# Two heads' value products by turns into the two halves of one PSUM bank, in both causal attentions of a two-layer trunk

## The chip, the core and the metric

One core of a Trainium2 chip runs the whole forward pass in one launch. The metric is device time in microseconds (us), the median of several executions. TensorE (PE in the profile, with PEld for its weight loads), VectorE (DVE), ScalarE (ACT) and GpSimd (POOL) have instruction streams of their own and wait for each other by semaphores. SyncE (SP) issues the loads from memory.

## The reference

Two layers over 512 tokens of width 1024. Each layer is a half-weighted feed-forward, a mixer, an attention over 256 memory tokens, and a second half-weighted feed-forward. The mixers hold the two causal attentions that are changed here: layer 0 a stick-breaking attention (8 heads of width 64, beside a gated branch), layer 1 a softmax attention with low-rank projections (16 heads, value width 64).

```python
for layer in range(DEPTH):
    x = x + 0.5 * _swiglu(_rmsnorm(x, ffn_pre_norm[layer]), ...)
    h = _rmsnorm(x, mix_norm[layer])
    if layer % 2 == 0:
        x = x + _even_mixer(h, ...)      # stick-breaking attention | gated branch, @ w_out
    else:
        x = x + _mla_mixer(h, ...)       # causal softmax attention, @ w_out
    x = x + _memory_cross_attention(...)
    x = x + 0.5 * _swiglu(_rmsnorm(x, ffn_post_norm[layer]), ...)

# stick breaking, per query block, strict = key position < query position
log_stay = jnp.where(strict, jax.nn.log_sigmoid(-z), 0.0)
log_rest = lax.cumsum(log_stay, axis=3, reverse=True) - log_stay
w = jnp.where(strict, jnp.exp(jax.nn.log_sigmoid(z) + log_rest), 0.0)
return jnp.einsum('bhqk,bkhd->bqhd', w, v)
# softmax
p = jax.nn.softmax(jnp.where(causal, sc, -jnp.inf), axis=-1)
return jnp.einsum('bhqk,bkhd->bqhd', p, v)
```

The last line of each attention is the value product that the change issues in another order.

## The kernel before

The residual stream lies on chip with features on partitions, as eight tiles of 128 x 512. Most products run as three passes of fp32r operands that were split into a high and a low part (`mm3`, lines 98 to 100). Weights come in granules (`gran`): a load, a rounded copy on ACT (line 79) and a difference on DVE or POOL (line 83).

The value products are different. Their operands are plain fp32, one product per key block j, four for a head, with 512, 384, 256 and 128 columns, since key block j meets only the queries from block j on. The stationary operand is v of one head, 128 keys x 64 features; what streams are the attention weights, keys on partitions. The result has 64 partitions. Heads of even number write partitions 0 to 63 of the accumulator `av`, heads of odd number partitions 64 to 127. A pair of heads fills the bank, and then ACT and DVE split it into the operands of the output projection (`obh`, `obl` in layer 0; `hh`, `hl` in layer 1).

**Layer 0, `stick`.** Per head `h`: `scores(h)` puts z for three units of key blocks into three PSUM banks; DVE adds the mask (line 359); ACT takes Abs, Exp and Ln (lines 416 to 418); DVE makes the softplus (line 419) and splits it into `th` and `tl` (lines 81, 83). `weights(h)` adds products of `th` and `tl` with triangular constants on TensorE (line 433), and ACT takes the Exp (line 436), which gives the weights. Between the two, `take(4)` twice draws eight steps of a filler: products that wait for nothing (the next pair's q and k, later half of the output projection). The value products of head h - 1 (line 444) stand between the two `take(4)` of step h. The filler is used up at the end.

**Layer 1, `mla_attn`.** In step n: `scores(n)` with the softmax (mask line 760, maximum 765, Exp 771, scaling 777), `weights(n - 1)`, which turns the weights by TensorE transposes (line 790) and copies them out of PSUM (ACT line 795 for units 0 and 1, DVE line 797 for unit 2), `turn` of head n + 2 (line 703), and `values(n - 1)` (line 808). Filler projections stand between them in steps 0 to 8. From there on early parts of the output projection fill in. All that the step issues on TensorE is held in written order by `queued()`, save products of the next stage.

A scheduler sets the order in which each engine's stream is written down: where the code does not bind it, it places an instruction by its own estimate of times. So a change on TensorE can also change the order on ACT and DVE.

Of the kernel before, what the change touches and what calls it, by code (L numbers as in the profile page):

```python
# [26 lines left out]
class Trunk:  # L27
    """The residual stream xT lives feature-major on chip; every product runs as
    three fp32r passes over operands split exactly into a high and a low part."""

    def __init__(self, ctx, tc, a, stop=None):
# [10 lines left out]
        # PSUM: two banks stay through all phases, which start in their own banks and end in these two,  # L42
        # so that no phase's first product waits for the last one's evacuation
# [3 lines left out]
    def queued(self):  # L47
        """What the block issues on the tensor engine comes behind what it had before."""
        return self.tc.issue_after(self.pe.ins)
# [9 lines left out]
    # ---------------------------------------------------------------- pieces  # L59
    def constants(self):  # L60
# [3 lines left out]
        # the first weights ahead of x: their split takes longer  # L64
# [10 lines left out]
    def split(self, hi, lo, src, eng_hi="act", eng_lo="dve"):  # L75
        """hi = src rounded to the multiplier's width, lo = src - hi (exact)."""
        nc = self.nc
        if eng_hi == "act":
            nc.scalar.copy(out=hi, in_=src)  # L79
        else:  # L80
            nc.vector.tensor_copy(out=hi, in_=src)
        e = nc.vector if eng_lo == "dve" else nc.gpsimd
        e.tensor_tensor(out=lo, in0=src, in1=hi.bitcast(F32), op=ALU.subtract)  # L83

    def gran(self, src, kt, cols, lo="pool"):
        """A weight granule [128, kt*cols] loaded and split."""
# [15 lines left out]
    def rsqrt(self, ssq, n, scale, eps, shape=None):  # L102
        """1/sqrt(ssq*scale + eps) on [128, n] by bit estimate and three Newton steps."""
# [13 lines left out]
    def prep(self, g, f):  # L117
        """Split gain*x_f for the next norm's consumers."""
# [12 lines left out]
    def squares(self, f):  # L131
        """Add the squares of x_f to the sums of the next norm."""
# [9 lines left out]
    def stats(self, pp, tag, bufs=None, bc=False):  # L142
        """rstd of every token: rc [128, NT] by token tile, and, if bc, rbc broadcast over partitions."""
# [28 lines left out]
    def out_half(self, ps, w, src, kh, first):  # L172
        """One half of the contraction of a pair of out_proj's output tiles, in steps."""
# [7 lines left out]
    def out_proj(self, pp, tag, w, src, order, g, begun=None):  # L181
        """x += src @ w by pairs of output tiles; w in granules [pair*2 + khalf] of [128, 4, 256].
        begun: accumulators that hold the first half already."""
# [15 lines left out]
    # ---------------------------------------------------------------- FFN  # L199
# [43 lines left out]
    # ---------------------------------------------------------------- token-major products  # L243
    def tok_chunk(self, pp, tag, grans):
        """h @ w for 256 columns, token-major: two banks of [128, 2, 256]."""
# [11 lines left out]
    # ---------------------------------------------------------------- layer 0's mixer  # L257
# [15 lines left out]
    def sgu(self, p, pp, v, og):  # L273
# [8 lines left out]
        # only s <= t mixes: partition s, free t  # L282
# [50 lines left out]
    def stick(self, p, pp, v, ob, src):  # L333
        """Stick-breaking attention, scores as [key, query]: causal blocks only."""
        nc, a = self.nc, self.a
        # key block -> (unit, column of its queries j*128.. in the unit); units are one bank each
# [9 lines left out]
        # -1 where row key >= column key  # L346
# [3 lines left out]
        # far below every score where key >= query: no softplus there, and no weight  # L350
# [10 lines left out]
        def proj(qk, pr, s):  # L361
            """q or k of a pair of heads, in steps."""
# [18 lines left out]
        def filler():  # L381
            """Products that wait for nothing, between the steps of the heads: the next pairs' q and k,
            and the part of the output projection that is fed by the gate."""
# [13 lines left out]
        def scores(h):  # L397
            """z of a head and the split softplus of its causal part."""
# [3 lines left out]
            for u in range(3):  # L402
# [8 lines left out]
                x2 = self.t(p, [P, n], f"t2{u}", bufs=2)  # L411
# [12 lines left out]
        def weights(st):  # L424
            """Suffix sums of the softplus, and the weights."""
# [12 lines left out]
        def values(h, st):  # L438
            if h % 2 == 0:
                self.av = self.t(pp, [P, S], "av", bufs=1)  # L440
            r = slice(h % 2 * 64, h % 2 * 64 + 64)
            for j in range(NT):
                u, o = AT[j]
                nc.tensor.matmul(self.av[r, j * P:], lhsT=v[:, j, h * 64:(h + 1) * 64], rhs=st[u][1][:, o:o + W[j]],
                                 start=(j == 0), stop=(j == NT - 1), skip_group_check=True)
            if h % 2 == 1:
                self.split(*ob[h // 2], self.av, "act", "dve")
# [6 lines left out]
        old = None  # L454
        for h in range(8):
            st = scores(h)
            take(4)
            if old is not None:
                values(h - 1, old)
            take(4)  # L460
            weights(st)
            old = st
        values(7, old)
# [3 lines left out]
    # ---------------------------------------------------------------- layer 1's mixer  # L467
    def rope_tables(self, p, op):
        """cos and sin of positions * inv_freq for [token, tile, 16], reduced modulo 2 pi by an
        exact digit scheme, and multiplied into the q and k gains of the two rope halves."""  # L470
# [59 lines left out]
    def mla(self):  # L530
        nc, tc, a = self.nc, self.tc, self.a
        H = 16
        with ExitStack() as outer:
# [20 lines left out]
            # the late tiles take the space of the stage before, so that the early ones need not wait for it  # L554
# [6 lines left out]
    def lora(self, p, pp, c, n, ss, cT, lg, j0):  # L561
        """rmsnorm of the token-major c [128, NT, n], turned feature-major and split."""
# [56 lines left out]
    def mla_attn(self, p, pl, pp, cT, krr, skr, gqk, neg, tq, o):  # L619
# [7 lines left out]
        def norms(st):  # L627
            """rstd of the heads' k (0) and q (1) from their sums of squares."""
# [484 lines left out]
```

## Time and profile before

| | us |
|---|---|
| median of 3 runs | 2326.71 |
| lowest, highest | 2326.22, 2329.08 |
| span of the profiled execution | 2328.0 |
| TensorE busy in it | 2274.4 (98%) |
| VectorE, ScalarE, GpSimd busy | 1018.2, 875.1, 903.4 |

The profile gives no time of the profiled execution apart from its span, 2328.0 us from the first to the last instruction, 1.3 us above the median of the runs. Its granted TensorE clock has a mean of 0.995 of full speed. In the rows a busy time is a union over time, and a record of a matrix product lasts from its start to the modelled end of its pipeline, so neighbours overlap; the distance from start to start is what TensorE spends on one.

### The profile page before, as it was taken

The page shows a single profiled execution, that of the slowest core. Times are in us where ns is not written, and L with a number is a line of the kernel's source. Part 1 is how long each engine was busy: PE and PEld are TensorE (multiplying, and loading weights), DVE is VectorE, ACT ScalarE, POOL GpSimd, SP SyncE. Part 2 cuts the span into 40 slices and gives each one's busy share as a digit, 9 for nine tenths or more (in the row PEclk, how much of TensorE's full clock was granted, in tenths as well). Part 3 has the DMA queues.
Part 4 walks back from the last instruction along what each step waited for, and adds up shares of the span by engine and source line. Part 5 has one row for each costly group of instructions (what it writes and reads, how often), then busy time and mean ns, then how long its engine had stood idle before and what let it go on. Part 6 is the DMA issues. An engine that isn't in the chain of part 4 may idle for free. (4 is left out here: it accounts for less than half of the span.)

```text
span 2328.0 us, 28369 instructions
## 1 busy us (share of the span) xinstructions
PE 2274.4 (98%) x11152; PEld 1891.5 (81%) x11152; DVE 1018.2 (44%) x1830; ACT 875.1 (38%) x1448; POOL 903.4 (39%) x441
## 2 busy tenths in 40 slices
PE   7999999999999999999999999998999999999999
PEld 6888888977988788888878888897768887888887
DVE  5322433465745533133343133368886545430330
ACT  4222233355644332232332223346655443322321
POOL 4444444201242444444544444434212323445443
PEclk9999999999999999999999999999999999999999
DMA  4223323311431232332322332321103313323322
GB/s 152 92 87 113 92 82 118 92 46 47 134 110 55 83 99 81 110 100 83 108 90 83 108 100 86 99 80 57 37 19 119 127 55 91 91 79 111 100 81 92
DMA packets 67350, 208.65 MB, mean 90 GB/s; under 512 B 8592, under 2 KB 10640, under 8 KB 67216
## 3 DMA queue, kind: packets, MB, share of 16 engines
q1 hardware_dynamic: 67216, 206.83, 29.1%
q8 instruction: 88, 1.44, 0.3%
q14 instruction: 46, 0.38, 0.1%
HBM read 204.70 MB, written 2.10 MB: 89 GB/s over the span
## 5 line engine op out<-in xcount | busy, mean ns | idle before, releaser
L83 POOL TENSOR_TENSOR wl<-wr,wh 128x1024 fp32r<-128x1024 f32 (+2 forms) x382 | 850.6, 2227 | 1253.0 <-ACT wh L79 1188.8
L79 ACT CAST wh<-wr 128x1024 fp32r<-128x1024 f32 (+3 forms) x423 | 408.7, 966 | 1029.8 <-PE mm L99 540.7
L98 PE MATMUL mm<-hh,wh 128*128 128x512 f32 x1440 | 562.8, 391 | 6.6 <-ACT hh L125 6.6
L100 PE MATMUL mm<-hh,wl 128*128 128x512 f32 x1440 | 562.5, 391 | 0.9 <-POOL wl L83 0.9
L99 PE MATMUL mm<-hl,wh 128*128 128x512 f32 x1440 | 562.2, 390 | 0.5 <-DVE hl L126 0.5
L98 PEld LDWEIGHTS mm<-hh,wh 128*128 128x128 f32 x1440 | 271.5, 189 | 62.9 <-ACT hh L125 6.6
L100 PEld LDWEIGHTS mm<-hh,wl 128*128 128x128 f32 x1440 | 271.6, 189 | 57.6 <-POOL wl L83 1.3
L99 PEld LDWEIGHTS mm<-hl,wh 128*128 128x128 f32 x1440 | 271.3, 188 | 57.6 <-DVE hl L126 1.0
L98 PE MATMUL A<-ah,wh 128*128 128x512 f32 x704 | 277.4, 394 | 0.0
L100 PE MATMUL A<-ah,wl 128*128 128x512 f32 x704 | 276.0, 392 | 0.0
L99 PE MATMUL A<-al,wh 128*128 128x512 f32 x704 | 273.2, 388 | 0.0
L222 DVE TENSOR_TENSOR t<-mm,rbc 128x512 f32<-128x512 f32 x88 | 60.8, 691 | 390.5 <-PE mm L100 390.5
L234 DVE SCALAR_TENSOR_TENSOR x<-A,x 128x512 f32<-128x512 f32 x64 | 44.3, 691 | 354.3 <-PE A L100 354.3
L83 DVE TENSOR_TENSOR al<-t,ah 128x512 fp32r<-128x512 f32 x88 | 160.8, 1828 | 59.1 <-ACT ah L79 59.1
L100 PEld LDWEIGHTS A<-ah,wl 128*128 128x128 f32 x704 | 132.1, 188 | 31.0
L99 PEld LDWEIGHTS A<-al,wh 128*128 128x128 f32 x704 | 132.2, 188 | 29.6
L98 PEld LDWEIGHTS A<-ah,wh 128*128 128x128 f32 x704 | 132.3, 188 | 26.4
L220 DVE TENSOR_TENSOR t<-mm,rbc 128x512 f32<-128x512 f32 x88 | 60.9, 692 | 117.1 <-PE mm L100 110.8
L126 DVE SCALAR_TENSOR_TENSOR hl<-x,gc,hh 128x512 fp32r<-128x512 f32 x64 | 82.8, 1307 | 36.7 <-ACT hh L125 36.6
L98 PE MATMUL A<-hh,wh 128*128 128x512 f32 x224 | 91.6, 410 | 0.7 <-ACT hh L79 0.7
L99 PE MATMUL A<-hl,wh 128*128 128x512 f32 x224 | 90.0, 402 | 0.0
L100 PE MATMUL A<-hh,wl 128*128 128x512 f32 x224 | 89.8, 401 | 0.0
(322 smaller groups left out, 3260.6 us busy)
## 6 DMA issues: line engine op xcount, KB each, us to landing
wr<-in_w_gu SPq DMA_DIRECT2D x176, 512.0 KB, 3.6
wr<-in_w_dn SPq DMA_DIRECT2D x64, 384.0 KB, 3.1
wr<-in_w_dn SPq DMA_DIRECT2D x64, 320.0 KB, 2.9
wr<-in_xmem_wkv SPq DMA_DIRECT2D x32, 512.0 KB, 3.2
wr<-in_xmem_wq SPq DMA_DIRECT2D x16, 512.0 KB, 3.3
wr<-in_xmem_wo SPq DMA_DIRECT2D x16, 512.0 KB, 3.2
wr<-in_sbg_w_zv SPq DMA_DIRECT2D x12, 512.0 KB, 3.5
wr<-in_sbg_w_qk SPq DMA_DIRECT2D x8, 512.0 KB, 3.6
```

What stands on the lines that cost most here:

```text
L79: nc.scalar.copy(out=hi, in_=src)
L83: e.tensor_tensor(out=lo, in0=src, in1=hi.bitcast(F32), op=ALU.subtract)
L98: mm(out, lhsT=A[0], rhs=B[0], start=start, stop=False, skip_group_check=True)
L99: mm(out, lhsT=A[0], rhs=B[1], start=False, stop=False, skip_group_check=True)
L100: self.pe = mm(out, lhsT=A[1], rhs=B[0], start=False, stop=stop, skip_group_check=True)
L126: nc.vector.scalar_tensor_tensor(out=hl, in0=self.x[f], scalar=col, in1=hh.bitcast(F32), op0=ALU.mult, op1=ALU.subtract)
L220: nc.vector.tensor_tensor(out=t1, in0=pg, in1=self.rbc, op=ALU.mult)
L222: nc.vector.tensor_tensor(out=t2, in0=pu, in1=self.rbc, op=ALU.mult)
L234: nc.vector.scalar_tensor_tensor(out=self.x[m], in0=ps, scalar=0.5, in1=self.x[m], op0=ALU.mult, op1=ALU.add)
```

## The change

`values` now takes a pair of heads and runs the key blocks outermost: for each j the product of the even head into partitions 0 to 63, then that of the odd head into partitions 64 to 127. It runs once the weights of both heads are there: in `stick` in steps h = 2, 4, 6 and after the last, in `mla_attn` in steps n = 2, 4, ..., 16. The number, the sizes and the operands of the products stay. `t2`, the buffer that holds layer 0's weights, has three buffers and not two, since the even head's weights live a step longer.

```diff
-                x2 = self.t(p, [P, n], f"t2{u}", bufs=2)
+                x2 = self.t(p, [P, n], f"t2{u}", bufs=3)
...
-        def values(h, st):
-            if h % 2 == 0:
-                self.av = self.t(pp, [P, S], "av", bufs=1)
-            r = slice(h % 2 * 64, h % 2 * 64 + 64)
+        def values(pr, sts):
+            av = self.t(pp, [P, S], "av", bufs=1)
             for j in range(NT):
                 u, o = AT[j]
-                nc.tensor.matmul(self.av[r, j * P:], lhsT=v[:, j, h * 64:(h + 1) * 64], rhs=st[u][1][:, o:o + W[j]],
-                                 start=(j == 0), stop=(j == NT - 1), skip_group_check=True)
-            if h % 2 == 1:
-                self.split(*ob[h // 2], self.av, "act", "dve")
+                for i, st in enumerate(sts):
+                    h = 2 * pr + i
+                    nc.tensor.matmul(av[i * 64:i * 64 + 64, j * P:], lhsT=v[:, j, h * 64:(h + 1) * 64],
+                                     rhs=st[u][1][:, o:o + W[j]], start=(j == 0), stop=(j == NT - 1),
+                                     skip_group_check=True)
+            self.split(*ob[pr], av, "act", "dve")
...
-            if old is not None:
-                values(h - 1, old)
+            if len(old) == 2:
+                values(h // 2 - 1, old)
+                old = []
             take(4)
             weights(st)
-            old = st
-        values(7, old)
+            old.append(st)
+        values(3, old)
...
-        def values(n, wT):
+        def values(n, wTs):
             g, h = divmod(n, G)
-            if n % 2 == 0:
-                self.av = self.t(pp, [P, S], "av", bufs=1)
-            r = slice((n % 2) * 64, (n % 2) * 64 + 64)
+            av = self.t(pp, [P, S], "av", bufs=1)
             for j in range(NT):
                 u, c0 = KA[j]
                 wd = S - j * P
-                self.pe = nc.tensor.matmul(self.av[r, j * P:], lhsT=gs[g]["v"][:, j, h, :],
-                                           rhs=wT[u][:, c0:c0 + wd], start=(j == 0), stop=(j == NT - 1), skip_group_check=True)
+                for i, wT in enumerate(wTs):
+                    self.pe = nc.tensor.matmul(av[i * 64:i * 64 + 64, j * P:], lhsT=gs[g]["v"][:, j, h + i, :],
+                                               rhs=wT[u][:, c0:c0 + wd], start=(j == 0), stop=(j == NT - 1),
+                                               skip_group_check=True)
...
             if old is not None:
+                wTs.append(wT)
+            if len(wTs) == 2:
                 with self.queued():
-                    values(n - 1, wT)
+                    values(n - 2, wTs)
+                wTs = []
```

On TensorE, in step h = 1 and h = 2 of layer 0 (`av` the accumulator, `t` the weights of a head, `v` the values, `A` and `wh` the filler's accumulator and weights). Before, head 0's four products stand in step 1:

```order
L100 MATMUL A_3638<-hh_423_2471,wl_3642 128x512
L444 MATMUL av_3734<-t_579_3604,v_2607 64x512
L444 MATMUL av_3734<-t_569_3574,v_2607 64x384
L444 MATMUL av_3734<-t_574_3589,v_2607 64x256
L444 MATMUL av_3734<-t_569_3574,v_2607 64x128
L98 MATMUL A_3638<-hh_433_2525,wh_3641 128x512
```

With the change step 1 has none, and step 2 has both heads' (`t_579` and `t_569` are head 0's, `t_601` and `t_591` head 1's):

```order
L445 MATMUL av_3842<-t_579_3604,v_2607 64x512
L445 MATMUL av_3842<-t_601_3712,v_2607 64x512
L445 MATMUL av_3842<-t_569_3574,v_2607 64x384
L445 MATMUL av_3842<-t_591_3682,v_2607 64x384
L445 MATMUL av_3842<-t_574_3589,v_2607 64x256
L445 MATMUL av_3842<-t_596_3697,v_2607 64x256
L445 MATMUL av_3842<-t_569_3574,v_2607 64x128
L445 MATMUL av_3842<-t_591_3682,v_2607 64x128
L98 MATMUL A_3746<-hh_433_2525,wh_3749 128x512
```

So two blocks of four have become one block of eight, at the place of the second.

On ScalarE in step h = 2 of layer 0 (`obh` the rounded copy of the finished accumulator of heads 0 and 1, line 418 the Ln of unit 2 of head 2). Before:

```order
L416 ACTIVATE t_623_3824<-z_3820 128x512
L417 ACTIVATE t_623_3824<-t_623_3824 128x512
L79 CAST obh_454_2599<-av_3734 128x512
L418 ACTIVATE t_623_3824<-t_623_3824 128x512
L79 CAST wh_4209<-wr_4207 128x1024
```

With the change:

```order
L416 ACTIVATE t_622_3819<-z_3815 128x512
L417 ACTIVATE t_622_3819<-t_622_3819 128x512
L418 ACTIVATE t_622_3819<-t_622_3819 128x512
L79 CAST obh_454_2599<-av_3842 128x512
L79 CAST wh_4204<-wr_4202 128x1024
```

The copy of the accumulator has moved behind the Ln. The same holds in steps 4 and 6, and on VectorE its partner `obl` stands behind `tl` of unit 2 and not ahead of the cast to `th`.

On TensorE at the end of layer 1's attention (`pt` the transposes of head 15's weights `pb`, `A` the output projection). Before, head 14's value products stand ahead of these transposes and head 15's behind:

```order
L790 MATMUL pt_14016<-ident_100,pb_2532_13958 128x128
L790 MATMUL pt_14016<-ident_100,pb_2530_13944 128x128
L808 MATMUL av_13997<-wT_2543_14007,vs_13264 64x512
L808 MATMUL av_13997<-wT_2545_14014,vs_13264 64x384
L808 MATMUL av_13997<-wT_2547_14019,vs_13264 64x256
L808 MATMUL av_13997<-wT_2545_14014,vs_13264 64x128
L98 MATMUL A_14035<-hh_2548_14025,wh_14069 128x512
```

With the change:

```order
L792 MATMUL pt_14011<-ident_100,pb_2530_13944 128x128
L810 MATMUL av_14016<-wT_2536_13983,vs_13264 64x512
L810 MATMUL av_14016<-wT_2542_14002,vs_13264 64x512
L810 MATMUL av_14016<-wT_2538_13990,vs_13264 64x384
L810 MATMUL av_14016<-wT_2544_14009,vs_13264 64x384
L810 MATMUL av_14016<-wT_2540_13995,vs_13264 64x256
L810 MATMUL av_14016<-wT_2546_14014,vs_13264 64x256
L810 MATMUL av_14016<-wT_2538_13990,vs_13264 64x128
L810 MATMUL av_14016<-wT_2544_14009,vs_13264 64x128
L98 MATMUL A_14035<-hh_2548_14025,wh_14069 128x512
```

Head 14's products no longer stand ahead of head 15's transposes; all eight are behind them.

## Rows read from the trace of the kernel before

**Rows 1.** The page's span and first part: busy time of each engine, share of the span, instructions.

```profile
span 2328.0 us, 28369 instructions
PE 2274.4 (98%) x11152; PEld 1891.5 (81%) x11152; DVE 1018.2 (44%) x1830; ACT 875.1 (38%) x1448; POOL 903.4 (39%) x441
```

**Rows 2.** The instructions of the accumulator `av`: count, shortest, median and longest record in ns, first and last start, shapes (partitions of the operand*columns of the stationary one, then what streams).

```profile
L808 PE MATMUL av<-wT,vs x128: 272/458/644, 1608.3 to 1748.3; 128*64 128x512 f32 x32, 128*64 128x384 f32 x32, 128*64 128x256 f32 x32, 128*64 128x128 f32 x32
L444 PE MATMUL av<-t,v x64: 272/432/643, 488.8 to 580.4; 128*64 128x512 f32 x16, 128*64 128x384 f32 x16, 128*64 128x256 f32 x16, 128*64 128x128 f32 x16
```

**Rows 3.** Busy time of each engine in three stretches: layer 0's attention from head 1's filler on, layer 1's attention with fillers, and its later heads. Columns: stretch, length, then busy us (instructions) by engine, granted TensorE clock, DMA share, GB/s.

```profile
486.00:583.00 97.00, 94.04 (x452) 69.81 (x453) 54.73 (x98) 50.78 (x98) 14.71 (x6) 1.00 0.14 42
1593.00:1690.00 97.00, 92.40 (x513) 72.12 (x513) 82.20 (x237) 68.03 (x169) 33.42 (x27) 1.00 0.11 39
1690.00:1751.00 61.00, 56.95 (x294) 38.48 (x294) 46.47 (x150) 33.83 (x87) 6.26 (x4) 1.00 0.07 22
```

**Rows 4.** TensorE's products in order of time around head 0's value products in layer 0. Columns: start us, length us, engine, line, operation; x8 is a merged run of eight records.

```profile
488.01 0.39 PE L98 MATMUL A<-hh,wh 128*128 128x512 f32 x1
488.24 0.39 PE L99 MATMUL A<-hl,wh 128*128 128x512 f32 x1
488.46 0.39 PE L100 MATMUL A<-hh,wl 128*128 128x512 f32 x1
488.78 2.37 PE L444 MATMUL av<-t,v 128*64 128x512 f32 x8
491.08 0.50 PE L98 MATMUL A<-hh,wh 128*128 128x512 f32 x1
491.42 0.40 PE L99 MATMUL A<-hl,wh 128*128 128x512 f32 x1
```

**Rows 5.** The weight loads of the same stretch, with the idle time before each in brackets.

```profile
488.78 0.19 PEld L444 LDWEIGHTS av<-t,v 128*64 128x64 f32 x2 [0.35 <-ACT t L418]
489.26 0.14 PEld L444 LDWEIGHTS av<-t,v 128*64 128x64 f32 x1 [0.29 <-issue]
489.69 0.14 PEld L444 LDWEIGHTS av<-t,v 128*64 128x64 f32 x1 [0.29 <-issue]
490.02 0.14 PEld L444 LDWEIGHTS av<-t,v 128*64 128x64 f32 x1 [0.19 <-issue]
490.34 0.57 PEld L444 LDWEIGHTS av<-t,v 128*64 128x64 f32 x3 [0.18 <-issue]
```

**Rows 6.** Whom TensorE waited for in layer 0's attention (471 to 583 us): us in total, times, longest.

```profile
PE z L433 <- DVE tl L83: 3.0, 3, 1.0
```

**Rows 7.** Step h = 2 of layer 0, in order of time: ACT, then DVE, then TensorE.

```profile
501.34 0.63 ACT L417 ACTIVATE t<-t 128x512 f32<-128x512 f32 x1
504.20 0.59 ACT L79 CAST obh<-av 128x512 fp32r<-128x512 f32 x1 [2.23 <-PE av L444]
504.68 0.63 ACT L418 ACTIVATE t<-t 128x512 f32<-128x512 f32 x1
...
505.35 0.69 DVE L419 SCALAR_TENSOR_TENSOR t<-z,t 128x512 f32<-128x512 f32 x1 [2.31 <-ACT t L418]
507.49 2.28 DVE L83 TENSOR_TENSOR tl<-t,th 128x512 fp32r<-128x512 f32 x1
...
509.82 0.50 PE L433 MATMUL z<-tl,negU 128*128 128x512 f32 x1 [1.00 <-DVE tl L83]
```

**Rows 8.** The last softplus part `tl` of an odd head on DVE, and its use on TensorE: heads 1 and 7 of layer 0.

```profile
490.19 0.69 DVE L83 TENSOR_TENSOR tl<-t,th 128x512 fp32r<-128x512 f32 x1
495.65 0.39 PE L433 MATMUL z<-tl,negU 128*128 128x512 f32 x1
...
573.03 0.69 DVE L83 TENSOR_TENSOR tl<-t,th 128x512 fp32r<-128x512 f32 x1
576.23 0.40 PE L433 MATMUL z<-tl,negU 128*128 128x512 f32 x1
```

**Rows 9.** Whom TensorE waited for in layer 1's attention (1593 to 1751 us).

```profile
PE pt L703 <- DVE wT L797: 3.8, 6, 1.7
PE pt L790 <- ACT wT L795: 3.0, 4, 1.2
PE pt L703 <- DVE qTl L83: 1.3, 1, 1.3
PE A L98 <- ACT hh L79: 0.7, 1, 0.7
```

**Rows 10.** The last scaled weights `pb` of two late heads of layer 1 on DVE, and the transposes that read them.

```profile
1714.09 0.35 DVE L777 TENSOR_SCALAR pb<-pb,asm 128x256 f32<-128x256 f32 x1
1716.09 1.04 PE L790 MATMUL pt<-ident,pb 128*128 128x128 f32 x8
...
1731.18 0.35 DVE L777 TENSOR_SCALAR pb<-pb,asm 128x256 f32<-128x256 f32 x1
1732.34 1.04 PE L790 MATMUL pt<-ident,pb 128*128 128x128 f32 x8
```

**Rows 11.** The end of layer 1's attention: head 14's value products, the last `pb` of head 15, its transposes, its value products.

```profile
1740.57 1.72 PE L808 MATMUL av<-wT,vs 128*64 128x512 f32 x4
1743.36 0.86 PE L808 MATMUL av<-wT,vs 128*64 128x256 f32 x4
...
1743.85 0.35 DVE L777 TENSOR_SCALAR pb<-pb,asm 128x256 f32<-128x256 f32 x1
...
1744.49 1.03 PE L790 MATMUL pt<-ident,pb 128*128 128x128 f32 x8
1746.18 2.37 PE L808 MATMUL av<-wT,vs 128*64 128x512 f32 x8
```

More of the change, by code (lines that the diff above doesn't have):

```diff
@@ L453, in stick @@
         take(2)
-        old = None
+        old = []
         for h in range(8):
@@ L457, in stick @@
             take(4)
-            if old is not None:
-                values(h - 1, old)
+            if len(old) == 2:
+                values(h // 2 - 1, old)
+                old = []
             take(4)
             weights(st)
-            old = st
-        values(7, old)
+            old.append(st)
+        values(3, old)
         self.run_all(fill)
@@ L807, in values @@
                 wd = S - j * P
-                self.pe = nc.tensor.matmul(self.av[r, j * P:], lhsT=gs[g]["v"][:, j, h, :],
-                                           rhs=wT[u][:, c0:c0 + wd], start=(j == 0), stop=(j == NT - 1), skip_group_check=True)
-            if n % 2 == 1:
-                f = n // 2
-                hi = self.t(self.hp, [P, S], f"hh{f}", F32R)
-                lo = self.t(self.hp, [P, S], f"hl{f}", F32R)
-                self.split(hi, lo, self.av, "act", "dve")
-                o.append((hi, lo))
+                for i, wT in enumerate(wTs):
+                    self.pe = nc.tensor.matmul(av[i * 64:i * 64 + 64, j * P:], lhsT=gs[g]["v"][:, j, h + i, :],
+                                               rhs=wT[u][:, c0:c0 + wd], start=(j == 0), stop=(j == NT - 1),
+                                               skip_group_check=True)
+            f = n // 2
+            hi = self.t(self.hp, [P, S], f"hh{f}", F32R)
+            lo = self.t(self.hp, [P, S], f"hl{f}", F32R)
+            self.split(hi, lo, av, "act", "dve")
+            o.append((hi, lo))
         take(LEAD2, False)
@@ L841, in mla_attn @@
             if old is not None:
+                wTs.append(wT)
+            if len(wTs) == 2:
                 with self.queued():
-                    values(n - 1, wT)
+                    values(n - 2, wTs)
+                wTs = []
             take(FILL[n][2])
```

## The prediction

> **What bounds the kernel now.** I read the page's busy times first: TensorE is busy 98% of the span, and no other engine reaches half of it [rows 1]. So what shortens TensorE's stream shortens the kernel, unless a stretch has another limit. Then the busy times of the stretches that the change touches [rows 3]. In layer 0's attention TensorE has 94.0 of 97 us and DVE only 54.7: TensorE is the limit. In layer 1's attention TensorE has 92.4 of 97 us, but DVE has 82.2, and in the later heads 57.0 against 46.5 of 61 us. There the head's softmax is close behind. The granted clock is 1.00 in all three, so TensorE is at its upper level, 2.4 GHz, throughout, and no clock effect is in the sum.
>
> The value products have 64 + 128 records for 32 + 64 products [rows 2]: each fp32 product runs as two passes, each with a weight load of its own. Around head 0's block [rows 4, 5] the filler's products before it start 0.23 us apart. Two loads of the 512-column passes come 0.43 us apart (489.26 and 489.69), the first ones 0.48, the 384-column passes 0.33. That is 0.43 / 512 = 0.84 ns a column. One head streams 2 x 1280 columns, 2.15 us. All that the block adds is 491.42 - 488.46 - 2 x 0.23 = 2.50 us: the time between the filler products on both sides, less their own two steps. So 0.35 us of it are its edges: 0.09 before the block, 0.05 for its first load (0.48 - 0.43), and the rest where the shape changes back, with the next filler step 0.34 in place of 0.23. A pair of heads costs 5.00 us today, and 12 pairs 60.
>
> **The change part by part.** *One block and not two.* One set of edges goes: 0.35 us a pair. That holds whatever else happens.
>
> *Neighbours in different halves.* The one open question is whether a product into partitions 64 to 127 can stream while one into 0 to 63 still does. They use different columns of the array and write different partitions. The trace before has no such neighbours, since the two heads of a pair always have other work between them, so I bound it.
>
> - No overlap: 2 x 2.15 + 0.35 = 4.65 us a pair, a gain of 0.35.
> - Full overlap: 2.15 + 0.35 = 2.50, a gain of 2.50.
> - Overlap with starts in program order: even pass 1, even pass 2, odd pass 1, odd pass 2, and so on. A pass waits for the one before it in its own half. Then the even head's second pass runs beside the odd head's first, the odd head's second beside the next key block's first, and so on. With 0.43, 0.32, 0.215 and 0.107 us for a pass of the four sizes, that is 3 x 0.43 + 2 x (0.32 + 0.215 + 0.107) = 2.57 us, with edges 2.92. If none of the seven changes of half hides its load, each adds the 0.05 of a first load: 3.27.
>
> I take the in-order case and the middle of its two ends, 3.1 us: a gain of **1.9 us a pair**. Starts in program order are what [rows 4, 5] show within one half, and nothing there lets a product pass another.
>
> The Trainium skill speaks for the overlap. "TensorEngine Tiling (Array Packing)", section Key Properties, says that tiles of the array work independently and can load weights and multiply in parallel, and that a change of tiling shape drains the engine; the edges in [rows 4] agree with the second part, and no row here shows the first.
>
> *The stall in layer 0.* Today ACT waits 2.23 us in step 2 for the end of the value products, because the copy of the accumulator stands ahead of the Ln that the next weights need. The softplus and its `tl` come late, and TensorE waits for them [rows 7], three times for 3.0 us in all [rows 6]. With the change the Ln and `tl` stand ahead of the copies, so this chain no longer hangs on the value products: 3.0 us go. Late next is `obh`, which only the output projection reads, steps later.
>
> *Cover that goes.* In the odd steps of layer 0 the 2.5 us of value products are gone from between scores and weights. Head 1's last `tl` ends at 490.88 and is read at 495.65, 4.8 us of slack; head 7's at 573.72 and 576.23, 2.5 us [rows 8]. Only head 7 comes near zero. I cost it at nothing.
>
> In layer 1 the odd steps lose 2.5 us too. The slack of late heads' `pb` is 1716.09 - 1714.44 = 1.65 and 1732.34 - 1731.53 = 0.8 us [rows 10], so TensorE will wait there for 1 to 2 us. On the other side TensorE already waits 8.8 us in this stage [rows 9], for copies out of PSUM, and in several steps the copies on ACT now stand ahead of the next Exp, which shortens those. Between all and nothing of the gain I take half, because in the first stretch DVE's 82.2 us leave at most 97 - 82.2 = 14.8 us at full use, and a stream in order does not reach that.
>
> *The last pair of layer 1.* Head 14's products cost nothing today: they run while head 15's softmax is made, whose last part ends at 1744.20, just before the transposes at 1744.49 [rows 11]. With the change all eight products stand behind those transposes. The end comes 3.1 - 2.5 = 0.6 us later.
>
> *The third buffer* of `t2` costs no instruction. Loads move by one place on their queue, and DMA is at 0.07 to 0.14 of its time here [rows 3].
>
> Sum: layer 0, 4 x 1.9 + 3.0 = 10.6. Layer 1, seven pairs x 1.9 = 13.3, half of it 6.65, less 0.6. Together 16.7 us. The span 2328.0 would become 2311.3; the median of the runs shown is 1.3 us lower, so from 2326.7 I say **2310 us**.
>
> **The rivals.** *Overlap, and layer 1 follows in full:* 10.6 + 13.3 - 0.6 = 23.3 us, 2303. For it speaks the new order of the copies; against it DVE's share. *Overlap, and layer 1 gives nothing:* 10.6 - 0.6 = 10, 2317.
>
> *No overlap.* The two halves share one stream. Then layer 0 gives 4 x 0.35 + 3.0 = 4.4, layer 1 half of 7 x 0.35 = 1.2, and the last pair costs 4.65 - 2.5 = 2.15: 3.4 us, 2323. For it speaks that the rows show no two products side by side in all of TensorE's work, against it that none had neighbours in different halves.
>
> *A change of half costs like a change of shape* (slower). If each of the seven changes in a pair drains what runs and shows its load, it costs the entry of a block, 0.09 + 0.05 = 0.14 us. A pair is then 4.65 + 7 x 0.14 = 5.63, 0.63 more than today. Twelve pairs cost 7.6, less the 3.0 of the stall, and the last pair loses its cover of 2.5: 7.1 us more, 2334. It decides from 0.35 / 7 = 0.05 us a change on. Within one half the loads speak against it [rows 5]: the next load starts with the running product and is hidden. Across the halves no row tells.
>
> The Trainium skill has a rule on that side: "TensorE: Matmul & The Clock Gate", section The mechanism, says that a weight load overlaps running products only where the row group differs; here both halves use all rows. By it the loads would show and this rival hold. The trace differs from that rule within one half, where loads into the same rows overlap [rows 5]; across the halves no run here shows it.
>
> **How the numbers follow.** Overlap 0.62 (as predicted 0.38, layer 1 in full 0.10, nothing from layer 1 0.14), no overlap 0.24, dear changes 0.14. The predicted time is that of the likeliest; its own range, with pairs between 2.9 and 3.3 us and a quarter to three quarters of layer 1, is 2304 to 2315. About 0.2% (4.7 us) can be told from no change here. Overlap is faster by more than that in nearly all its cases; no overlap is within it for more than half (2323 is 3.4 us down), faster for a third, slower for the rest; dear changes are slower. Faster 0.62 x 0.98 + 0.24 x 0.35 = 0.69; slower 0.13 + 0.02 = 0.15; the same 0.16. For 8 in 10 the range reaches from 2300, below which part of the fullest case lies (0.04), to 2327, above which the dear changes and the worst of no overlap lie (0.15).
>
> **What would show it.** Loads and starts inside a block: with overlap the odd head's first pass starts within some 0.05 us of the even head's second, and a block of 16 records spans 2.6 to 2.9 us. Without it the block spans 4.3 to 4.4, and with dear changes over 5. In layer 0 the three waits for `tl` should be gone from the list of waits, and ACT's Ln of unit 2 should not follow a wait for `av`. In layer 1 the waits for DVE and ACT tell how much of the gain was kept, and the gap ahead of head 15's transposes should be 2 us or so. I am wrong if the block shows another pattern than these, or if layer 0 shows a new wait in the odd steps.

## The result, and the profile after

The changed kernel takes **2312.5 us** (median of 4 runs, 2311.2 to 2314.3), the kernel before 2327.9 beside it (2326.2 to 2329.5): a ratio of 0.9931, 95% interval 0.9917 to 0.9945. The prediction said 2310, in 2300 to 2327. In a second set beside other versions it took 2311.4 against 2329.1 (0.9918, 0.9904 to 0.9932). The time is as predicted, but of the terms in its sum only the edges measured as costed: the others are off in both directions, and that they add up to nearly the right total is luck.

The page of the kernel after, span and busy times, to be read against [rows 1]:

```profile
span 2310.4 us, 28373 instructions
PE 2252.6 (98%) x11152; PEld 1884.6 (82%) x11152; DVE 1015.5 (44%) x1830; ACT 875.7 (38%) x1448; POOL 903.2 (39%) x441
```

TensorE has 21.8 us less work in its records for the same 11152 instructions, the other engines nearly the same. The span lost 17.6 us. Where a run's time and its span are both on record, the time is 1.7 us above the span (2312.07 and 2310.4 here), so the profiled execution of the kernel before was longer than its median; the medians differ by 15.4 us.

**The block.** TensorE's products around the first pair in layer 0, to be read against [rows 4], and then the weight loads, against [rows 5]. Columns as there.

```profile
499.35 0.39 PE L100 MATMUL A<-hh,wl 128*128 128x512 f32 x1
499.66 2.37 PE L445 MATMUL av<-t,v 128*64 128x512 f32 x16
501.97 0.50 PE L98 MATMUL A<-hh,wh 128*128 128x512 f32 x1
502.30 0.40 PE L99 MATMUL A<-hl,wh 128*128 128x512 f32 x1
```

```profile
499.66 0.20 PEld L445 LDWEIGHTS av<-t,v 128*64 128x64 f32 x4 [0.35 <-issue]
500.14 0.14 PEld L445 LDWEIGHTS av<-t,v 128*64 128x64 f32 x2 [0.28 <-issue]
500.57 0.14 PEld L445 LDWEIGHTS av<-t,v 128*64 128x64 f32 x2 [0.28 <-issue]
500.90 0.14 PEld L445 LDWEIGHTS av<-t,v 128*64 128x64 f32 x2 [0.18 <-issue]
501.22 0.58 PEld L445 LDWEIGHTS av<-t,v 128*64 128x64 f32 x6 [0.18 <-issue]
```

Sixteen records now last 2.37 us, as long as eight did before. Where one head had one load it now has two in the same 0.14 us: the single records show each pass of the odd head 6 ns behind the same pass of the even head. Both halves stream at once, and a pair costs 502.30 - 499.35 - 0.46 = 2.49 us, as one head did.

Nine of the twelve blocks last 2.37 or 2.38 us. Layer 0's last one takes 3.13, because head 7's products wait there for the Exp on ACT that makes their weights:

```profile
566.84 3.13 PE L445 MATMUL av<-t,v 128*64 128x512 f32 x16
567.59 0.29 PEld L445 LDWEIGHTS av<-t,v 128*64 128x64 f32 x4 [0.57 <-ACT t L436]
```

Layer 1's seventh takes 3.37 (its odd head waits for a copy of `wT`) and its last 4.00, at half clock.

**The two stages.** Busy times of each stage (columns as in [rows 3]), layer 0 from its first scores to 2.4 us after its last value product, layer 1 from its first scores to the first product of the next stage; the kernel before:

```profile
472.04:583.10 111.06, 107.87 (x521) 80.60 (x521) 63.82 (x117) 59.41 (x115) 14.71 (x6) 1.00 0.16 46
1594.38:1750.98 156.60, 148.30 (x799) 109.80 (x797) 127.72 (x384) 101.35 (x253) 38.38 (x28) 1.00 0.10 32
```

and of the kernel after, with two stretches of 4 us inside layer 1:

```profile
472.42:572.40 99.98, 97.59 (x517) 76.93 (x517) 62.67 (x116) 59.92 (x115) 15.27 (x6) 1.00 0.17 51
1584.52:1735.09 150.57, 136.08 (x799) 105.21 (x797) 127.44 (x384) 101.49 (x253) 38.15 (x28) 0.97 0.10 34
1680.00:1684.00 4.00, 4.00 (x17) 3.22 (x17) 3.82 (x13) 2.77 (x8) 1.79 (x1) 0.60 0.17 67
1728.00:1732.00 4.00, 3.74 (x12) 1.45 (x14) 0.42 (x1) 0.70 (x2) 0.00 (x0) 0.57 0.00 0
```

Layer 0 is 11.1 us shorter: TensorE lost 10.3 us of work and 0.8 of idle time. Of the work, 0.9 us only changed its place: four products of the output projection, 0.23 us each, stood ahead of head 7's value products and now stand behind them (521 records and 517). From the first scores to the first product of `mm` behind the projection the change is worth 10.2 us (472.04 to 612.76 before, 472.42 to 602.99 after). Layer 1 is 6.0 us shorter: 12.2 us less work, but 14.5 us idle where it was 8.3, and a mean granted clock of 0.97 where it was 1.00.

Whom TensorE waited for most, in layer 0 (against [rows 6]) and then in layer 1 (against [rows 9]), us in total, times, longest:

```profile
PE z L433 <- DVE tl L83: 2.2, 2, 1.1
```

```profile
PE pt L705 <- DVE wT L799: 5.2, 9, 0.8
PE pt L792 <- ACT wT L797: 3.8, 4, 2.2
PE pt L792 <- DVE asm L775: 2.4, 1, 2.4
PE pt L792 <- DVE qTl L83: 1.7, 2, 1.1
```

The waits for `tl` have not gone. They have moved from heads 2, 4 and 6 to heads 3 and 5. In layer 1 there are new waits ahead of the transposes of the weights (L792) where value products stood ahead of them before and do not any more; the longest two last over 2 us.

**Who holds `tl`.** Head 3 in layer 0, in order of time, on GpSimd, VectorE and TensorE:

```profile
515.07 2.64 POOL L83 TENSOR_TENSOR wl<-wr,wh 128x1024 fp32r<-128x1024 f32 x1 [8.12 <-ACT wh L79]
...
515.50 2.75 DVE L83 TENSOR_TENSOR tl<-t,th 128x512 fp32r<-128x512 f32 x1
...
518.31 0.50 PE L433 MATMUL z<-tl,negU 128*128 128x512 f32 x1 [1.11 <-DVE tl L83]
```

VectorE needs 0.69 us for this `tl` [rows 8], and here 2.75. GpSimd is making the low part of a weight granule at that time; its operation ends at 517.71, and `tl` 0.54 us later, as if it had only then begun. The same stands in [rows 7], unread by me: head 2's `tl` took 2.28 us there, and GpSimd's row of the kernel before is

```profile
506.69 2.52 POOL L83 TENSOR_TENSOR wl<-wr,wh 128x1024 fp32r<-128x1024 f32 x1 [41.83 <-DVE obl L83]
```

until 509.21, with `tl` from 507.49 to 509.77. And the longest wait but one in layer 1, in order of time on VectorE, GpSimd, ACT and TensorE:

```profile
1675.64 2.37 POOL L83 TENSOR_TENSOR wl<-wr,wh 128x1024 fp32r<-128x1024 f32 x1 [11.72 <-ACT wh L79]
...
1676.02 2.03 DVE L106 TENSOR_SCALAR rs_v<-ssqk 128x32 f32<-128x32 f32 x1
...
1678.14 0.78 ACT L773 ACTIVATE pb<-lg,anm,sqr 128x512 f32<-128x512 f32 x1 [2.58 <-DVE anm L769]
...
1679.54 0.44 PE L792 MATMUL pt<-ident,pb 128*128 128x128 f32 x2 [2.16 <-ACT wT L797]
```

A 128x32 operation takes 2.03 us and ends 0.04 us behind GpSimd's; ACT's Exp waits behind it, TensorE behind that, and the stretch 1680 to 1684 follows at a clock of 0.60.

### The profile page after: what moved, and what is told of

Its sections match the earlier page's. It is cut to its first block, busy times and chain, and to the rows that moved or that the text cites. A ratio compares the mean times of both kernels' runs of the same rounds, so it can differ in the third digit from the quotient of the medians.

```text
span 2310.4 us, 28373 instructions
## 1 busy us (share of the span) xinstructions
PE 2252.6 (98%) x11152; PEld 1884.6 (82%) x11152; DVE 1015.5 (44%) x1830; ACT 875.7 (38%) x1448; POOL 903.2 (39%) x441
```

## The experiments

My theory after this first look: the overlap is whole, and what it does not bring is lost in waits that the move to every second step opens. Layer 0 and layer 1 below mean the length of the stage, from its first scores to the end of its last value product in layer 0 and to the next stage in layer 1, against the trace of the kernel before (in layer 0 the 0.9 us that only changed place are part of every figure but e3's); the time is the median, with the ratio to the kernel before in the same set (2327.9 to 2330.8 over the sets).

| version | layer 0 | layer 1 | time | ratio (95%) |
|---|---|---|---|---|
| changed kernel | -11.1 | -6.0 | 2312.5 | 0.9931 (0.9917-0.9945) |
| the same, second set | -11.1 | -6.0 | 2311.4 | 0.9918 (0.9904-0.9932) |
| e1 one head after the other | -5.6 | +3.9 | 2329.0 | 0.9997 (0.9988-1.0006) |
| e2 layer 0 alone | -11.1 | +0.3 | 2318.6 | 0.9944 (0.9927-0.9961) |
| e3 layer 1 alone | 0.0 | -6.2 | 2321.8 | 0.9960 (0.9946-0.9975) |
| e4 filler in odd steps | -11.1 | -6.8 | 2313.6 | 0.9935 (0.9918-0.9952) |
| e5 last pair apart | -11.1 | -7.3 | 2312.0 | 0.9923 (0.9908-0.9938) |
| e6 filler 6 and 2 | -14.2 | -6.3 | 2307.6 | 0.9908 (0.9889-0.9928) |
| e8 block in two steps | -8.0 | -11.3 | 2310.5 | 0.9912 (0.9893-0.9931) |
| e9 = e6 + e8 | -14.2 | -11.7 | 2305.3 | 0.9893 (0.9879-0.9907) |
| e10 = e9, low parts on VectorE | -14.2 | -8.4 | 2306.4 | 0.9898 (0.9883-0.9912) |
| e11 low parts in four | -13.8 | -8.3 | 2302.9 | 0.9882 (0.9864-0.9899) |
| e12 = e9 + e11 | -14.2 | -13.9 | **2298.8** | 0.9862 (0.9844-0.9879) |

**e1: the same blocks, one head after the other.**

```
-            for j in range(NT):
-                for i, st in enumerate(sts):
+            for i, st in enumerate(sts):
+                for j in range(NT):
```

> The changed kernel, but inside a pair's block all four products of the even head come first, then all four of the odd head; place of the block and all else as in the change. Theory A (halves overlap only where their products stand next to each other): the block, 2.38 us in the change, grows to about 4.65 us. Layer 0 loses 4 x 2.2 = 9 us against the change. Layer 1 loses up to 8 x 2.2 = 18 us, less what of its new waits in the odd steps is made good by nothing here, so the whole is some 25 us above the change, 2330 to 2340. Theory B (each half has a stream of its own and takes its products whenever it is free): the block stays near 2.4 us and the time at 2312. Theory C (the gain comes from the move alone, one block and other orders on ACT and DVE): the time is that of the change within 3 us although the block takes 4.65 us.

The time is that of the kernel before: with the block in place but not by turns, nothing is won. None of the three theories had this block. The first pair's block, products and loads:

```profile
499.19 0.39 PE L100 MATMUL A<-hh,wl 128*128 128x512 f32 x1
499.50 3.93 PE L445 MATMUL av<-t,v 128*64 128x512 f32 x16
503.36 0.50 PE L98 MATMUL A<-hh,wh 128*128 128x512 f32 x1
503.70 0.40 PE L99 MATMUL A<-hl,wh 128*128 128x512 f32 x1
```

```profile
500.74 0.14 PEld L445 LDWEIGHTS av<-t,v 128*64 128x64 f32 x1 [0.18 <-issue]
501.06 0.62 PEld L445 LDWEIGHTS av<-t,v 128*64 128x64 f32 x6 [0.19 <-issue]
501.98 0.14 PEld L445 LDWEIGHTS av<-t,v 128*64 128x64 f32 x1 [0.29 <-issue]
```

Neither side by side (2.37) nor one after the other (4.3 to 4.4): 3.93, which is 1.56 us more than 2.37. And 1.56 us into the block, at 501.06, single loads become a group of six: there the odd head's first pass starts, beside the even head's third key block. So the odd head starts while two products ahead of it in the program are unfinished, and no sooner. It did not wait for its weights, whose last Exp ended at 495.14, and in all twelve blocks of e1 the odd head starts beside the even head's third key block. A pair costs 503.70 - 499.19 - 0.46 = 4.05 us, 0.95 less than two blocks. In layer 1, eight pairs should give 7.6 us; the stage is 3.9 longer. The move to every second step alone thus costs some 11.5 us there. That is where the changed kernel's gain goes as well.

**e2 and e3: one layer alone.** The other attention's code is that of the kernel before.

> The change in layer 0 alone; layer 1 as before. Theory A (the two layers have separate limits, and each keeps in the end what its stage shows: layer 0's stage was 11.1 us shorter in the changed kernel's trace, layer 1's 6.0): 2328.5 - 11 = 2317.5, and layer 0's block of 16 records 2.30 us long. Rival B (most of the gain is made in one layer and shows up elsewhere): 2312 or 2326.

> The change in layer 1 alone; layer 0 as before. Theory A (the layers add up; layer 1's TensorE waits for the copies of the weights out of PSUM and keeps 6 of the 20 us that its blocks save): 2328.5 - 6 = 2322.5. Rival B (layer 1 starts at another place in its loads in the changed kernel, and without layer 0's part it keeps the 9 us of my fuller case, or nothing): 2319 or 2328.

Theory A holds in both. Stage by stage the parts add up: -11.1 and -6.2 alone, -11.1 and -6.0 together. In times, 2318.6 and 2321.8 against 2327.9 to 2330.8 are 9 to 12 and 6 to 9 us. Layer 1's small gain is its own.

**e4 and e5: more cover in layer 1's odd steps.** e4 moves a filler step out of the even steps into the odd ones; e5 issues head 14's products a step earlier again.

```
-        FILL = [(0, 1, 1)] + [(1, 0, 1)] * 8 + [(0, 0, 0)] * 8
+        FILL = [(0, 1, 1)] + [(1, 1, 1), (1, 0, 0)] * 4 + [(0, 0, 0)] * 8
```

> The changed kernel with layer 1's filler projections moved from even to odd steps (three in steps 1, 3, 5, 7, one in steps 2, 4, 6, 8; the total stays). Theory: of 20 us that the eight blocks of layer 1 save, 14 were given back because the odd steps lost the cover of the softmax; a third projection there (2 us) covers again, the waits of 0.8 to 1.2 us ahead of the transposes of line 792 in steps 3, 5 and 9 go, and the time falls by 2 to 5 us. Rival: DVE is the limit of that stretch (82 of 97 us before); then the waits move to the copies out of PSUM and the time stays within 1 us.

> The changed kernel, but in layer 1 the last pair (heads 14 and 15) is issued one head at a time, head 14 a step earlier, as before the change. Theory: the 2.55 us wait ahead of head 15's transposes and the lower granted clock behind it (0.57 of full speed over the four us of the last block) come from head 14's missing cover; with it back the wait falls to 0.5 us or less, the clock stays at 1.00, and the time falls by 2 to 4 us. Rival: the softmax of head 15 sets that time alone and the clock falls all the same; then within 1 us of the change.

Neither moves the time by more than the sets differ. In e4 the waits change places (for the copies of `wT`, 5.2 + 3.8 = 9.0 us in the changed kernel and 10.4 in e4). In e5 the wait of 2.4 us for `asm` and the clock's fall at 1728 go, as in its theory, and the stage gains 1.3 us; that is a net figure, since heads 14 and 15 no longer run side by side there, which is worth 2.5 us a pair.

**e6: layer 0's filler drawn by 6 and 2.** The second draw of the filler takes six steps in odd heads, which have no value products, and two in even ones.

```
-            take(4)
+            take(6 if h % 2 else 2)
```

> The changed kernel with layer 0's filler moved from even to odd steps (ten steps of filler in odd heads, six in even ones, where it was eight each). Theory: the two waits of 1.3 us for tl in heads 3 and 5 come from the value products that no longer stand in the odd steps; 1.4 us more filler there takes them away, and the time falls by 2 to 2.6 us. Rival: tl is late for its own sake (2.3 us of DVE in place of 0.7, beside POOL), and the wait comes back in the even steps; then within 1 us.

3.1 us more, and TensorE is busy in all of the stage:

```profile
472.44:569.20 96.76, 96.76 (x517) 76.71 (x517) 61.70 (x116) 59.76 (x115) 14.36 (x6) 1.00 0.18 53
```

Every `tl` takes 0.69 us or less here; what lies under GpSimd's operation now is `qkl`, for which TensorE does not wait. So this run cannot tell more cover from less collision. e11 can.

**e8: layer 1's block in two steps.** Key block 0 of both heads at the end of the even step, key blocks 1 to 3 a step later.

```
+            if late is not None:
+                with self.queued():
+                    values(n - 3, late, (1, 2, 3))
+                late = None
             if len(wTs) == 2:
                 with self.queued():
-                    values(n - 2, wTs)
+                    values(n - 2, wTs, (0,) if n < 16 else range(NT))
+                late = wTs
```

> The changed kernel, but in layer 1 the pair's block is cut in two: key block 0 of both heads (2 of the 8 products, 0.86 us of the 2.15) at the end of the even step, key blocks 1 to 3 (1.29 us) a step later, so that both steps have value products between the scores and the next transposes. The buffers of the copied weights of units 1 and 2 go from two to three, those of the low part of q from three to two. Theory A (layer 1 loses most of its gain because the odd steps have no value products, and TensorE waits there, 1.23 + 1.16 + 0.84 + 2.34 + 2.55 = 8.1 us in the changed kernel, for the softmax and the copies): the odd steps get 1.3 us of cover each, some 5 us of these waits and the stretch at half clock behind the longest go, less 7 more edges of 0.35 us: 2306 to 2310. Rival B (the chain of copies and softmax on DVE and ACT limits two heads together, wherever the products stand): the waits move and only the edges show, 2312 to 2315.

Layer 1 gives 11.3 us and not 6.0, although each pair has one more set of edges. TensorE's waits there, and the stage:

```profile
PE pt L705 <- DVE wT L799: 3.8, 6, 0.9
PE pt L792 <- ACT wT L797: 3.2, 3, 1.9
PE pt L705 <- ACT wT L797: 2.2, 3, 1.2
PE pt L792 <- DVE asm L775: 0.7, 1, 0.7
```

```profile
1590.73:1736.06 145.33, 133.90 (x799) 102.42 (x797) 125.98 (x384) 100.75 (x253) 38.16 (x28) 0.99 0.10 35
```

Idle time falls from 14.5 to 11.4 us and the clock is back at 0.99. The time does not show it: the four runs lie between 2306.4 and 2315.5, and the median, 2310.5, is not clear of the changed kernel's. The profiled execution was the longest of the four; layer 0, whose code is unchanged, had a stretch at half clock in it (0.57 from 546 to 554), and its -8.0 in the table, in place of -11.1, is that. So e8's worth is read from layer 1's stage alone, and that theory A holds is shown there and not in the time.

**e9: both edits, beside the changed kernel.**

> The changed kernel itself once more, in 5 rounds, so that the two versions beside it are compared under the same conditions: 2310 to 2315, as before.

> The changed kernel with both edits that paid in their stages: layer 0's second take of the filler draws 6 steps in odd heads and 2 in even ones, and layer 1's block of a pair is cut in two over two steps. Theory A (the stages add up: layer 0 gave 3.1 us more with the one edit, layer 1 5.3 us more with the other): 2312 - 8.4 = 2304, 2302 to 2306; no wait of TensorE in layer 0's attention. Rival B (what layer 1 gains is taken back by clock drops elsewhere): 2307 to 2309.

2305.3 against 2311.4 in the same set, and the two kernels' runs do not overlap (2303.6 to 2306.2, 2309.8 to 2311.5). The stages give what they gave alone.

**e10: four low parts on VectorE.**

> As the version with both edits, but the low parts of the first four granules of layer 1's output projection are made on VectorE and not on GpSimd. In the changed kernel a 128x32 operation of VectorE took 2.03 us there (0.17 elsewhere) and ended 0.04 us after the low part that GpSimd made at the same time; ACT waited 2.58 us for VectorE and TensorE 2.34. Theory A (VectorE's small operation is held by GpSimd's, and that makes TensorE's longest wait): no VectorE operation over 1.5 us there, the wait of 2 us or so goes, and with it the stretch at half clock behind it (0.60 over 4 us, worth some 1.6 us); VectorE pays 1.2 us for each low part instead. 2 to 3 us faster than the version with both edits. Rival B (VectorE is the limit of the stage, whoever holds it): the wait stays, the time is within 1 us.

Right on the mechanism and wrong on the time. `rs_v` takes 0.17 us and the wait behind it is gone, but VectorE now makes four low parts of 1.2 us or more (1.8 the longest), and TensorE waits for VectorE's copies instead:

```profile
PE pt L705 <- DVE wT L799: 9.1, 6, 4.1
```

**e11 and e12: GpSimd's low parts in four pieces.** Same engine, same work, shorter operations, for the granules of the two attentions and the output projections.

```
+        if eng_lo == "pool4":
+            n = lo.shape[-1] // 4
+            for i in range(4):
+                c = slice(i * n, (i + 1) * n)
+                e.tensor_tensor(out=lo[:, c], in0=src[:, c], in1=hi.bitcast(F32)[:, c], op=ALU.subtract)
+            return
```

> The changed kernel, but GpSimd makes the low part of each granule of the two attentions and their output projections in four operations of a quarter of the columns and not in one. Order and work on the other engines stay. In the changed kernel's trace each VectorE operation with all its operands in SBUF that starts while GpSimd works on a low part (2.4 us) ends behind it: tl of heads 3 and 5 of layer 0 took 2.75 us and not 0.69, a 128x32 operation in layer 1 2.03 us and not 0.17, and TensorE's longest waits follow on these. Theory A (VectorE is held until GpSimd's operation ends): it is then held for a quarter as long at most, about 0.6 us; the two waits of layer 0 (1.33 and 1.30 us) go, the wait of 2.34 us in layer 1 falls below 1 us and the stretch of 0.60 clock behind it goes: 3 to 6 us, 2306 to 2309. Rival B (the two only share a rate, and as much of GpSimd's work in pieces slows VectorE as much): tl stays at 2 us or more, and the time within 1.5 us of 2311.5. Rival C (GpSimd takes its next piece before VectorE gets its turn): the same as B in time, with VectorE ending behind the last piece.

> The version with both edits (layer 0's second take by 6 and 2, layer 1's block cut in two), and GpSimd's low parts in four operations as in the run beside it. Theory A: layer 0 has no wait left to win; in layer 1 the wait of 2.1 us at the last norms and one of 1.2 go in part: 2 to 3 us, 2302 to 2304. Rivals B and C: 2305 within 1.5 us.

Theory A, with more than I expected: 8.5 us for e11 (against 2311.4), 6.5 for e12 over e9 (2298.8). The pieces on GpSimd, the three `rs_v` of layer 1 and all `tl` of layer 0 in e11 (shortest, median, longest in ns):

```profile
L87 POOL TENSOR_TENSOR wl<-wr,wh x25: 722/737/1201, 504.6 to 574.8; 128x256 fp32r<-128x256 f32 x25
...
L112 DVE TENSOR_SCALAR rs_v<-ssqk x3: 366/387/389, 1589.8 to 1668.7; 128x32 f32<-128x32 f32 x3
...
L89 DVE TENSOR_TENSOR tl<-t,th x24: 415/682/1118, 479.2 to 562.2; 128x512 fp32r<-128x512 f32 x16, 128x256 fp32r<-128x256 f32 x8
```

The longest `tl` is 1.12 us and not 2.75, `rs_v` 0.39 and not 2.03, while a piece takes 0.74: VectorE is held until the running piece ends, and then gets its turn. GpSimd pays for it, 934.2 us busy in all where it was 903.2; ACT waits for its pieces three times, 6.9 us in all, but TensorE waits for none of them. Layer 0 gains 2.7 us with the old filler order, which settles e6: without the collision the two waits for `tl` are gone and only 0.2 us, for `th`, is left. One part of the expectation failed: in layer 1 e11's clock still falls twice, behind a wait of 1.6 us for `pb` (0.57 from 1678 to 1682) and at the last block, so that the stage's mean is 0.98. A third of the gain, 3.1 us, comes between the attentions: a wait of TensorE of 3.0 us for `prk`, at 1562 to 1565 in the changed kernel, is 0.6. It was there in the kernel before as well, and has nothing to do with the change. Part of the 3.1 us may be the clock: in the changed kernel it was 0.57 from 1564 to 1572, behind that wait, and in e11 it was 1.00 there.

## Why the prediction was right, and where it was not

**Two products side by side: right, and mis-sized.** The step that failed is "overlap with starts in program order", where a pass waits for the odd half's turn. I reasoned from one half, where nothing overtakes. Two halves have their passes side by side, 6 ns apart, and e1 shows an odd product starting with two products ahead of it unfinished. The term was 1.9 us a pair and measured 2.5; the edges, 0.35, were right. Over 12 pairs that would be 30 us in place of 23. By the prediction's own signs, too, it was another pattern: the odd head starts with the even head's first pass and not its second, and the block spans 2.37 us and not 2.6 to 2.9.

The Trainium skill's page "TensorEngine Tiling (Array Packing)", section Key Properties, had it right that tiles work independently. The rule of the Trainium skill's page "TensorE: Matmul & The Clock Gate", section The mechanism, that loads overlap running products only where the row group differs, does not hold here: both halves use all rows, yet the pair of loads at 500.14 and all behind it lie beside running products (499.66 to 502.03), and the first four loads take 0.20 us where two took 0.19 [rows 5].

**Layer 0: 10.6 predicted, 10.2 measured, by two errors that cancel.** The blocks gave 9.2 and not 7.6 (four times 2.5, less the 0.76 us that the last one waits inside). The stall gave 0.8 and not 3.0. The step that failed is the cause of the stall: I put it on the copy that stood ahead of the Ln. The copy made `tl` late by 2.2 us, but it was GpSimd's operation, into which `tl` then fell, that held it for 1.6 us more; without that, `tl` would have ended at about 508.2 and TensorE, which had no other work from 508.8 on, would not have waited. I had the 2.28 us in [rows 7] and the 0.69 in [rows 8] before me and did not ask why they differ. For the same reason "cover that goes: nothing" failed: the slack of heads 1 and 7 is 4.8 and 2.5 us, but heads 3 and 5 met GpSimd's operation. A new wait in the odd steps was one of the prediction's signs of being wrong, and it came. Nor did the prediction have a term for the last block, which stands straight behind head 7's weights.

**Layer 1: 6.05 predicted, 6.0 measured, for a wrong sum.** Half of 13.3 less 0.6 is by chance what is left of 20. Of the 20 us, 6.2 went into new idle time, 1.0 into the wait inside the seventh block, and some 5 into half clock, though the prediction had no clock effect in its sum: in the stretch from 1680, 0.60 over 4 us means 3.2 us at 1.2 GHz, which cost 1.6; a third such stretch lies at 1640, and each comes behind waits of 1.0 to 2.4 us. Some 2 us I can't assign. The step that failed is the half: it was a choice between all and nothing, reasoned from VectorE's busy time. The rival "DVE is the limit" was weak: e12 takes the stage from 156.6 to 142.7 us with VectorE about as busy (123.8 us, 127.7 before), and part of VectorE's 82.2 us in [rows 3] was time held by GpSimd, such as 1.84 us for one 128x384 scaling that takes 0.42 elsewhere. What limited the changed kernel was that its odd steps have nothing to run while the copies are made (e8 gives 5 us back), and the collisions (e11, 2.3 us).

**The last pair: wrong.** I costed 0.6 us for head 14's products behind head 15's transposes; against e5, where head 14 stands apart as before, it is 1.3. The wait ahead of those transposes grew to 2.4 us, as I had listed it (2 us or so), but the clock fell behind it (0.57 from 1728 on), and the block took 4.00 us where the same one takes 2.37 in layer 0. TensorE's rows of after, against [rows 11]:

```profile
1726.62 1.35 PE L792 MATMUL pt<-ident,pb 128*128 128x128 f32 x8 [2.38 <-DVE asm L775]
1728.26 0.45 PE L792 MATMUL pt<-ident,pb 128*128 128x128 f32 x2 [0.29 <-ACT wT L797]
1728.65 4.00 PE L810 MATMUL av<-wT,vs 128*64 128x512 f32 x16
```

e5 took both away, and lost the pair's overlap for it.

**The rivals.** "No overlap" and "dear changes" are refuted by the block; e1 shows that without turns the change is worth nothing (2329.0). Layer 1 gave neither all nor nothing.

## What to carry to other kernels

Two fp32 products with 64-column weights run at the same time when they write different partition halves and are issued by turns, and both then cost what one did; but products that are gathered into every second step leave the other step without cover, so spread the gathered block over both. Before a stall is put down to an order, compare the duration of each operation in its chain with the same operation elsewhere: the long ones among short ones that I traced here were held by another engine, and cutting that engine's operations into pieces was worth 8.5 us, half as much as the change itself.

## What the runs showed of the hardware that I had not expected

- A VectorE operation on two operands in SBUF, or a tensor_scalar there, that starts under a GpSimd tensor_tensor ends 0.01 to 0.56 us behind it: some 140 such operations in the kernel before and as many in the one after, counted among those that start with 0.9 us or more of GpSimd's operation to go. Some 40 others in each ended in their usual time under it; nearly all of these read PSUM (`qTl` 0.68, the mask 0.42) or are reductions, reciprocals and statistics. The Trainium skill's page "SBUF — State Buffer", section Who interferes with whom, states it: such operations need the ports that the two engines share, and whoever starts first holds them for its whole instruction. The trace agrees (`tl` 2.75 us in place of 0.69), and e11 shows that four short operations let VectorE in between.
- A product in one half started while two earlier ones of the other half were unfinished, and did not while three were (e1: 1.56 us into a block whose third key block starts at 1.55, in eleven of the twelve blocks; in the twelfth, part of which ran at half clock, at 2.70 and 2.69).
- Half clock behind waits of 1.0 to 2.4 us appeared in layer 1 of the changed kernel three times and not at all before, where the longest wait is 1.7 us [rows 9]; in e12, whose longest wait there is 1.3 us, the stage's clock is 1.00. A wait of that length does not always bring it: e9 has one of 1.9 us left and stays at 1.00.
